# A third group of blocks in seven products in the last two gate-and-up stages, 64 instead of 48 pre-added weight blocks' transfers, and fixed PSUM banks

## The chip, the cores and the metric

The kernel runs on one core of a Trainium2 chip as a single launch. The metric is device time in microseconds. Before the change three runs took 997.59, 998.87 and 999.01 us, so the median is 998.87 us. The execution that the profiler recorded took 996.52 us, and the span from its first to its last instruction is 994.7 us.

## What is computed

Two decoder layers run on 256 tokens of width 1024 in float32. Each layer is a feed-forward net (added with factor 0.5), a token mixer (causal pooling beside attention), and a second feed-forward net. The feed-forward net is the part that the change touches:

```python
D_MODEL, SEQ, DEPTH, D_FF = 1024, 256, 2, 2816

def rms_norm(x, g):
    xf = x.astype(jnp.float32)
    y = xf * lax.rsqrt(jnp.mean(xf * xf, axis=-1, keepdims=True) + EPS)
    return (y * g.astype(jnp.float32)).astype(x.dtype)

def swiglu(h, w_gate_up, w_down):
    a, b = jnp.split(h @ w_gate_up, 2, axis=-1)
    return (jax.nn.silu(a) * b) @ w_down

    x = x + 0.5 * swiglu(rms_norm(x, ffn1_norm), ffn1_w_gate_up, ffn1_w_down)
    ...                     # the mixer
    x = x + 0.5 * swiglu(rms_norm(x, ffn2_norm), ffn2_w_gate_up, ffn2_w_down)
```

## The kernel before

**Number format.** Each float32 operand is split into two float32r parts, `hi` and `lo`. A product is made of hi by hi, hi by lo and lo by hi. Weights come from DRAM in units of 1 MB (128 partitions x 2048 floats). A unit is loaded into a tile `raw` (4 buffers) by a transfer that SP issues; ScalarE copies each half to `hi`; VectorE subtracts and writes `lo` (`split`, lines 186 to 188, for plain units; lines 176 and 177 for sum forms). `hi` and `lo` have six half-size buffers each, which is three units. A load for unit i therefore waits until the split of unit i-4 has read `raw`, and a split of unit i waits until TensorE is done with unit i-3. `unit()` hands out the next split unit, `fetch()` starts the following one.

**Stages.** There are four feed-forward stages: stage 0 (which begins the program), stage FU, stage LU and stage LU+FU. The mixer stands between 0 and FU and between LU and LU+FU. Each stage has 22 gate-and-up blocks (128 columns of the gate and 128 of the up matrix) and then 11 down units. In stage 0 every block is computed plainly: `pair` multiplies one unit with the normed activations `hx` (32 matmuls, PSUM tile `ps`), and `drain` moves the result to `ab` (one ScalarE copy, one VectorE add). `post` then scales with the norm, applies SiLU, multiplies and splits two blocks for the down product (tiles `ga`, `gb`, `gc`, `gd`).

**Seven products.** In stages FU, LU and LU+FU two groups of four blocks, A (blocks 12 to 15) and B (blocks 18 to 21), are computed in the Strassen-Winograd manner: tokens and the 1024 inputs are each halved, and seven products (`strassen`, forms "1" to "7", 16 matmuls each, `by_tokens`) stand in for the four pairs. Their left sides are the activations' halves and four sums of them (`x_forms`, made once a stage after block 2, tiles `pre`, `vt`, `sf`); their right sides are three quadrants of the weights (forms 1, 2, 3) and four sums of quadrants (7, 6, 5, 4). Results are kept by tokens in PSUM (tiles `pxA`, `pyA`, `pzA`), go through `tk`, get SiLU and product in `gated` (ScalarE writes `sg`, VectorE writes `vt`), and are turned back by TensorE transposes into `pt` in `turned` (four transposes for two blocks; a ScalarE copy and a VectorE subtraction then write `gd` or `gb`).

**Weight sums in DRAM.** The four sums of quadrants are built in DRAM by accumulating transfers on POOL's queue, ahead of their stage: `go_on` issues the next step, held back by a dependency on the last VectorE operation in the list `marks`. A group needs eight steps: for form 7 a copy and an accumulation from `w`, for form 6 a copy of sum 7 (`f<-f`) and an accumulation, for form 5 a copy and an accumulation, for form 4 a copy of sum 6 (`f<-f`) and an accumulation. Six groups make 48 steps. SP then loads a sum like a unit (`raw<-f`).

**Order.** TensorE runs in program order (`keep`); the framework's scheduler places the other engines' instructions between, and each engine runs its list in order. The order of a stage's pairs and forms is the list of `feed_order`: a number is a pair, "1A" is form 1 of group A:

```python
return [0, 1, "1A", 2, "2A", 3, 4, "7A", 5, "6A", 6, "5A", 7, "4A", "3A", 8, "1B", 9, "2B", 10, "7B", 11, "6B", 16,
        "5B", 17, "4B", "3B"]
```

After "3A" follow pair 8, the transposes for two blocks, form "1B", the first half of pair 9, the transposes of the other two blocks. PSUM tiles of the pool `pat` (4 banks) are taken in turn. The down product comes right after, and group B's transposes stand inside it.

Of the kernel before, what the change touches and what calls it, by code (L numbers as in the profile page):

```python
# [18 lines left out]
F32 = mybir.dt.float32  # L19
# [6 lines left out]
P = 128  # L26
# [17 lines left out]

FU = NF + NF // 2 + 24
LU = FU + NF + NF // 2
GROUPS = {"A": 12, "B": 18}
XF = 2
SHIFT = 16
RAW = {"1": "11", "2": "21", "3": "22"}  # L50
SUMS = (("7", "12", "22"), ("6", "7", "11"), ("5", "11", "12"), ("4", "6", "21"))


def feed_order():

    return [0, 1, "1A", 2, "2A", 3, 4, "7A", 5, "6A", 6, "5A", 7, "4A", "3A", 8, "1B", 9, "2B", 10, "7B", 11, "6B", 16,
            "5B", 17, "4B", "3B"]


def feed_units(base):  # L60
    return [base + n if isinstance(n, int) else (base, n) for n in feed_order()]


C_G1, C_GM, C_G2, C_BG, C_PS, NG = 0, 8, 16, 24, 40, 44
# [3 lines left out]
def trunk_kernel(ctx: ExitStack, tc: tile.TileContext, x_in, w_in, pw_in, qkn_in, rope_in, mask_in, band_in, out):  # L68
# [12 lines left out]
    def quarter(name):  # L81
        return pat.tile([P, 2, S], F32, name=name, tag="at")
# [64 lines left out]
        return z.rearrange("p (i c) -> p i c", i=2)  # L147

    def far_sums(base):
        steps_left.extend((base, g, f, src, kw) for g in GROUPS for f, one, two in SUMS  # L150
                          for src, kw in ((one, {}), (two, {"accum_op": OP.add})))

    def go_on():
# [241 lines left out]
    def bc2(a):  # L395
        return a.unsqueeze(1).to_broadcast([P, 2, a.shape[-1]])

    def ffn(after, n0=0, end=False, col=None, base=0, far_at=()):
        gs, gt = {}, {}

        def room(name, n0, m):
# [53 lines left out]
        if n0:  # L455
# [6 lines left out]
            for i in range(n0 + 1, NF + 1):  # L462
                if i < NF:
                    pair(unit(), wide(i))
                    fetch()
                    if i >= 8 and i % 3 == 2:
                        go_on()
                if i == NF or i % 3 != 1:
                    for n in range(done, NF if i == NF else min(done + 2, i - 1), 2):
                        scaled = post(n)  # L470
                        done = n + 2
                        if i == n0 + 1:
                            behind(scaled, drained[-1])
        else:
# [6 lines left out]
            columns(ws[1], pss[1], range(4, NK))  # L481
            drain(wide(1), pss[1])

            pre = acts.tile([P, 12 * S], F32, name="pre", tag="gb")
            vt = acts.tile([P, 2, GW], F32, name="vt", tag="v")
            tk = {g: acts.tile([P, 2, GW], F32, name="tk", tag="tok", bufs=2) for g in GROUPS}
# [56 lines left out]

            def turned(n, g):

                pt = quarter("pt")
                for i in range(2):
                    for t in range(2):
                        keep(nc.tensor.transpose(pt[:, i, t * P:(t + 1) * P], gq[2 * t + n][:, i * P:(i + 1) * P], ident))  # L549
                name, i = place(GROUPS[g] + 2 * n)  # L550
                g = gt[name][:, i:i + 2]
                act(g[:, :, 0, :], pt, AF.Copy)
                tt(g[:, :, 1, :], pt, g[:, :, 0, :].bitcast(F32), op=OP.subtract)

            bank = {}

            def strassen(f, g):

                b = ("x" if f in "1653" else "z" if f == "2" else "y") + g
                if b not in bank:  # L560
                    bank[b] = quarter("p" + b).rearrange("p a s -> p (a s)")
                z = bank[b]
# [19 lines left out]
            due = None  # L582
            wait = [0, 1]
            for n in feed_order()[2:]:
                if isinstance(n, str):
                    strassen(*n)
                    if n[0] == "3":
                        due = n[1]
                    continue
                if due == "A0":  # L590
                    pair(unit(), wide(n), lambda: turned(0, "A"), NK // 2)
                    due = None
                else:
                    pair(unit(), wide(n))
                fetch()
                if due == "A":
                    turned(1, due)
                    due = "A0"
# [8 lines left out]
            if due:  # L607
                last = {(1, 0): lambda: turned(1, due), (1, 5): lambda: turned(0, due)}
# [23 lines left out]
    def add_x(f, ps, two, r):  # L632
        t = x[:, f, :]
        if two:
            t = small.tile([P, S], F32, name="t", tag="sg", bufs=2)
            act(t, ps[:, 1, :], AF.Copy)
            if r is not None:
                tt(t, ps[:, 0, :], t, op=OP.add)
                stt(t, t, 0.5, r, op0=OP.mult, op1=OP.mult)
                marks.append(tt(x[:, f, :], x[:, f, :], t, op=OP.add))  # L640
                return
            stt(t, t, 0.5, x[:, f, :], op0=OP.mult, op1=OP.add)
        stt(x[:, f, :], ps[:, 0, :], 0.5, t, op0=OP.mult, op1=OP.add)

    def tokens():
# [362 lines left out]
    for l in range(L):  # L1008
        l_of[0] = l
        if l == 0:  # L1010
            for base in STAGES:
                far_sums(base)
        ffn(lambda f: prep(f, l, C_GM), len(w3) if l == 0 else 0, col=C_G1, base=l * LU, far_at=(1, 3, 5, 7, 9))
        if l == 0:
            for d, z in ((rope, rope_in), (mask, mask_in), (qkn, qkn_in)):
                nc.sync.dma_start(d, z)
        mix(l, lambda f: prep(f, l, C_G2))
        if l + 1 < L:
            ffn(lambda f: prep(f, l + 1, C_G1), col=C_G2, base=FU, far_at=(1, 3, 5, 7, 9))
# [92 lines left out]
```

## Time and profile before

| what | value |
|---|---|
| median of three runs | 998.87 us |
| profiled execution | 996.52 us (span 994.7 us) |
| TensorE busy | 989.5 us, 99% |
| VectorE busy | 801.1 us, 81% |
| ScalarE busy | 651.4 us, 65% |
| loads by SP, 16 DMA engines' time | 57.9% |
| transfers by POOL, 16 DMA engines' time | 21.2% |
| gate-and-up part of stage LU | from 508 to 622 us |
| gate-and-up part of stage LU+FU | from 825 to 941 us |

"Busy" is the time in which an engine executed something; on TensorE it counts overlapped matmuls as well. Durations of neighbouring instructions overlap by some hundredths of a us, so the pitch (start to start) is a little shorter than the duration. A row of the chain of waits gives start, length, engine, tile, line and the number of instructions. In a timeline row the bracket at the end is the idle time ahead of the instruction and what ended it.

### The profile page before, as it was taken

To read this page: it belongs to the slowest core of one execution; us is meant where nothing else is said; L and a number is where in the kernel's file an instruction comes from. 1 tells how busy PE (TensorE), PEld (TensorE's weight loads), DVE (VectorE), ACT (ScalarE), POOL (GpSimd) and SP (SyncE) were. 2 spreads that over 40 slices of the span, in tenths; PEclk is the share of its full clock that TensorE was granted. 3 is DMA by queue.
4 is the path that set the end of the run, shared out by engine and by line. 5 is a ranking of instruction groups with operands and counts; after the bars stand their busy time and mean duration, and the time that the engine had idled before them with its cause. 6 is when DMAs were issued, how large, how long until landed. Compare 5 with 4: busy or idle time off the path is not lost.

```text
span 994.7 us, 16119 instructions
## 1 busy us (share of the span) xinstructions
PE 989.5 (99%) x6312; PEld 898.6 (90%) x6312; DVE 801.1 (81%) x1136; ACT 651.4 (65%) x974; POOL 55.8 (6%) x95
## 2 busy tenths in 40 slices
PE   9999999999999999999999999999999999999998
PEld 8998888898899988889988889888989998888897
DVE  6987777698978799886779888676988888988862
ACT  7865555567756787675578677555677568776641
POOL 0000001002100100000000000000021000000000
PEclk9999999999999999999999999999999999999999
DMA  8878899964889999798966979897858895787740
GB/s 298 319 259 284 249 306 294 293 195 182 275 249 308 351 286 335 251 336 261 300 240 244 299 270 308 304 282 265 261 184 251 268 296 207 260 291 254 254 148 22
DMA packets 45243, 262.11 MB, mean 263 GB/s; under 512 B 4400, under 2 KB 5680, under 8 KB 22448
## 3 DMA queue, kind: packets, MB, share of 16 engines
q1 hardware_dynamic: 34992, 210.76, 57.9%
q0 software_dynamic: 10176, 50.33, 21.2%
q8 instruction: 49, 0.80, 0.3%
q14 instruction: 26, 0.21, 0.1%
HBM read 260.03 MB, written 51.38 MB: 313 GB/s over the span
## 4 chain that ended last, share of the span: by engine, by line
PE 99%; DMA 0%; ACT 0%; DVE 0%; SPq 0%; issue 0%
PE ps L99 72%; PE pt L99 7%; PE two L99 4%; PE pxB L99 3%; PE pxA L99 3%; PE pyA L99 2%; PE pyB L99 2%; PE pe L99 1%; PE sc L99 1%; PE pzB L99 1%; PE pzA L99 1%; PE pt L549 1%; PE pt L739 1%; PE y L99 1%; DMA raw<-w 0%; PE tp L695 0%
## 5 line engine op out<-in xcount | busy, mean ns | idle before, releaser
L188 DVE TENSOR_TENSOR lo<-raw,hi 128x1024 fp32r<-128x1024 f32 (+2 forms) x319 | 378.2, 1197 | 112.5 <-ACT hi L187 110.8
L187 ACT ACTIVATE hi<-raw 128x1024 fp32r<-128x1024 f32 (+2 forms) x319 | 327.8, 1036 | 198.6 <-PE ps L99 126.0
L99 PE MATMUL ps<-hx,hi 128*128 128x512 f32 x1312 | 443.2, 384 | 0.6 <-ACT hi L187 0.6
L99 PE MATMUL ps<-hx,lo 128*128 128x256 f32 x1312 | 358.7, 273 | 0.0
L99 PEld LDWEIGHTS ps<-hx,hi 128*128 128x128 f32 x1312 | 246.2, 188 | 44.6 <-ACT hi L187 0.8
L99 PEld LDWEIGHTS ps<-hx,lo 128*128 128x128 f32 x1312 | 246.5, 188 | 0.3 <-DVE lo L188 0.3
L177 DVE TENSOR_TENSOR lo<-raw,hi 128x1024 fp32r<-128x1024 f32 x84 | 102.2, 1221 | 23.8 <-ACT hi L176 23.7
L176 ACT ACTIVATE hi<-raw 128x1024 fp32r<-128x1024 f32 x84 | 88.9, 1059 | 46.8 <-PE ps L99 31.5
L99 PE MATMUL ps<-ga,hi 128*128 128x512 f32 (+1 forms) x264 | 87.9, 378 | 0.0
L99 PE MATMUL ps<-ga,lo 128*128 128x256 f32 x256 | 70.0, 273 | 0.0
L161 POOL DMA_DIRECT2D f<-w x36 | 33.3, 937 | 594.9 <-DVE ab L237 288.1
L99 PE MATMUL ps<-gb,hi 128*128 128x512 f32 (+1 forms) x198 | 65.4, 376 | 0.0
L99 PE MATMUL pt<-hi,hx 128*128 128x512 f32 x192 | 65.1, 385 | 0.0
L99 PEld LDWEIGHTS ps<-ga,hi 128*128 128x128 f32 x264 | 49.0, 188 | 8.3
L99 PE MATMUL pt<-lo,hx 128*128 128x256 f32 x192 | 52.6, 274 | 0.0
L99 PE MATMUL ps<-gb,lo 128*128 128x256 f32 x192 | 52.4, 273 | 0.0
L99 PEld LDWEIGHTS ps<-ga,lo 128*128 128x128 f32 x256 | 48.1, 188 | 0.0
L99 PE MATMUL ps<-gc,hi 128*128 128x512 f32 (+1 forms) x132 | 44.3, 376 | 0.0
L99 PE MATMUL ps<-gd,hi 128*128 128x512 f32 (+1 forms) x132 | 44.3, 376 | 0.0
L99 PE MATMUL ps<-mk,hi 128*128 128x256 f32 x256 | 44.1, 275 | 0.0
L237 DVE TENSOR_TENSOR ab<-ps,ab 128x512 f32<-128x512 f32 x62 | 42.4, 684 | 0.0
L99 PEld LDWEIGHTS ps<-gb,hi 128*128 128x128 f32 x198 | 36.7, 188 | 6.2
(251 smaller groups left out, 1585.1 us busy)
## 6 DMA issues: line engine op xcount, KB each, us to landing
raw<-w SPq DMA_DIRECT2D x170, 1024.0 KB, 6.9
f<-w POOLq DMA_DIRECT2D x36, 1024.0 KB, 11.8
raw<-f SPq DMA_DIRECT2D x24, 1024.0 KB, 5.5
raw<-w SPq DMA_DIRECT2D x16, 256.0 KB, 5.3
out_dram<-gx SPq DMA_DIRECT2D x8, 128.0 KB, 2.0
gx<-x SPq DMA_DIRECT2D x3, 256.0 KB, 5.6
qk<-pw SPq DMA_DIRECT2D x2, 256.0 KB, 4.7
gx<-x SPq DMA_DIRECT2D x1, 300.0 KB, 2.8
```

The source lines that it names most:

```text
L99: return keep(nc.tensor.matmul(*args, **kw))
L161: z = nc.gpsimd.dma_start(two_rows(far[f, g, base]), src, **kw)
L176: act(hv, a, AF.Copy)
L177: tt(lv, a, hv.bitcast(F32), op=OP.subtract)
L187: act(hi, w, AF.Copy)
L188: return tt(lo, w, hi.bitcast(F32), op=OP.subtract)
L237: drained.append(tt(t, ps[:, :, 0, :], t, op=OP.add))
L549: keep(nc.tensor.transpose(pt[:, i, t * P:(t + 1) * P], gq[2 * t + n][:, i * P:(i + 1) * P], ident))
L739: keep(nc.tensor.transpose(pt[:, h, o * P:(o + 1) * P], pr[:, h, c * P:(c + 1) * P], ident))
```

## The change

In stages LU and LU+FU a third group of four blocks (8 to 11, now called B; blocks 18 to 21 are now C) is computed in seven products. Stage FU keeps two groups, A and C. The order of a stage is a table: `TWO` for stage FU is the old order with "t1A" and "t0A" naming the transposes; `THREE` for the other two has 10 pairs and 21 forms. An entry such as `(6, "t0A")` is pair 6 with the transposes in its middle.

```diff
-GROUPS = {"A": 12, "B": 18}
+GROUPS = {"A": 12, "B": 8, "C": 18}
...
+TWO = (0, 1, "1A", 2, "2A", 3, 4, "7A", 5, "6A", 6, "5A", 7, "4A", "3A", 8, "t1A", "1C", (9, "t0A"), "2C", 10, "7C", 11, "6C",
+       16, "5C", 17, "4C", "3C")
+THREE = (0, 1, "1A", 2, "2A", 3, "1B", 4, "7A", "6A", 5, "5A", "4A", "3A", (6, "t0A"), "t1A", "7B", "6B", "2B", 7, "5B", "1C",
+         "4B", "3B", (16, "t0B"), "t1B", "7C", "6C", "2C", 17, "5C", "4C", "3C")
+FEED = {FU: TWO, LU: THREE, LU + FU: THREE}
...
-        late_r = not end
+        late_r = True
...
-                    if i >= 8 and i % 3 == 2:
+                    if i >= 8 and i % 2 == 0:
                         go_on()
...
+            three = FEED[base] is THREE
+            tk = {g: acts.tile([P, 2, GW], F32, name="tk", tag="tok", bufs=2) for g in ("AB" if three else "AC")}
+            tk.setdefault("C", tk["A"])
+            banks4 = [quarter(f"b{i}").rearrange("p a s -> p (a s)") for i in range(4)]
+            for g in groups_of(base):
+                for f in "1653":
+                    bank[f + g] = banks4[0 if (g == "B" if three else g == "A") else 2]
+                bank["2" + g] = banks4[1]
+                bank["7" + g] = banks4[3]
+                bank["4" + g] = banks4[1 if three else 3]
...
-                pt = quarter("pt")
+                if g == "C":
+                    pt = quarter("pt")
+                else:
+                    pt = banks4[1 if three or n else 0].rearrange("p (a s) -> p a s", s=S)
...
-                by_tokens(f, z, f in "127")
+                z = bank[f + g]
+                by_tokens(f, z, f in "127" or three and f == "4")
...
                 elif f == "5":
                     act(p1, z, AF.Copy)
-                    tt(p1, bank["y" + g], p1, op=OP.add)
+                    tt(p1, bank["7" + g], p1, op=OP.add)
                     gated(p1, 1, 1, 1)
+                    if three:
+                        tt(w, bank["7" + g], w, op=OP.add)
...
-                if n in (6, 11):
+                if n in steps_at:
                     go_on()
...
+        elif r is not None:
+            z = small.tile([P, S], F32, name="t", tag="sg", bufs=2)
+            stt(z, ps[:, 0, :], 0.5, r, op0=OP.mult, op1=OP.mult)
+            tt(t, t, z, op=OP.add)
+            return
...
-        ffn(..., far_at=(1, 3, 5, 7, 9))
+        ffn(..., far_at=(0, 1, 3, 4, 6, 7, 9), steps_at=(3, 6, 16))
-            ffn(lambda f: nc.sync.dma_start(out[:, f, :], x[:, f, :]), end=True, col=C_G2, base=LU + FU)
+            ffn(lambda f: nc.sync.dma_start(out[:, f, :], x[:, f, :]), end=True, col=C_G2, base=LU + FU, steps_at=(3, 6))
```

Form 4 gets a start of its own in bank 1 in the three-group stages, where it was added onto form 7's bank before; the missing sum is made up by one more VectorE addition after form 5 (line 596). Eight groups need 64 steps, and the places at which `go_on` is called now come to 64 (54 before, 48 of them used). In the last stage the norm's factor is now put on the gate half alone ahead of SiLU and on the down sums at the end, as it was in the other stages.

In the rows that follow, line numbers of the changed kernel are higher: 199 is the plain split (188 before), 188 the split of a form (177), 248 the drain (237), 562 the product in `gated` (541), 577 the split after a transpose (553), 593 and 600 the additions of forms 5 and 4 (574 and 579). `b_5315` to `b_5318` are the four fixed banks of stage LU.

VectorE's list in stage LU, from the end of `x_forms` on; before:

```order
L541 SCALAR_TENSOR_TENSOR vt<-tk,sg 128x256
L237 TENSOR_TENSOR ab<-ps,ab 128x512
L506 TENSOR_TENSOR sf<-vt,sf 128x512
L177 TENSOR_TENSOR lo<-raw,hi 128x2x2x256
L188 TENSOR_TENSOR lo<-raw,hi 128x1024 x2
```

and in the changed kernel:

```order
L562 SCALAR_TENSOR_TENSOR vt<-tk,sg 128x256
L248 TENSOR_TENSOR ab<-ps,ab 128x512
L527 TENSOR_TENSOR sf<-vt,sf 128x512
L199 TENSOR_TENSOR lo<-raw,hi 128x1024
L188 TENSOR_TENSOR lo<-raw,hi 128x2x2x256 x4
L199 TENSOR_TENSOR lo<-raw,hi 128x1024
L248 TENSOR_TENSOR ab<-ps,ab 128x512
```

Where the second half of 7A's split stood, the second half of pair 4's split stands now, and the splits of 7A and 6A follow as a run of four.

VectorE's list in stage LU around the end of group A, from the additions of form 5 or 4 to the first split after a transpose; before (the end of form 1B, pair 9 and form 2B are split in it):

```order
L579 TENSOR_TENSOR tk<-pyA,tk 128x512
L177 TENSOR_TENSOR lo<-raw,hi 128x2x2x256
L541 SCALAR_TENSOR_TENSOR vt<-tk,sg 128x256
L188 TENSOR_TENSOR lo<-raw,hi 128x1024
L541 SCALAR_TENSOR_TENSOR vt<-pxA,sg 128x256
L188 TENSOR_TENSOR lo<-raw,hi 128x1024
L443 TENSOR_TENSOR ab<-ab,r 128x2x256
L177 TENSOR_TENSOR lo<-raw,hi 128x2x2x256
L448 TENSOR_TENSOR ab<-ab 128x2x256
L177 TENSOR_TENSOR lo<-raw,hi 128x2x2x256
L237 TENSOR_TENSOR ab<-ps,ab 128x512
L553 TENSOR_TENSOR gd<-pt,gd 128x2x256
```

and in the changed kernel (pair 6 and forms 7B and 6B are split in it):

```order
L199 TENSOR_TENSOR lo<-raw,hi 128x1024 x2
L593 TENSOR_TENSOR tk<-b_5318,tk 128x512
L596 TENSOR_TENSOR tk<-b_5318,tk 128x512
L188 TENSOR_TENSOR lo<-raw,hi 128x2x2x256
L562 SCALAR_TENSOR_TENSOR vt<-tk,sg 128x256
L600 TENSOR_TENSOR tk<-b_5316,tk 128x512
L188 TENSOR_TENSOR lo<-raw,hi 128x2x2x256 x2
L562 SCALAR_TENSOR_TENSOR vt<-tk,sg 128x256
L562 SCALAR_TENSOR_TENSOR vt<-b_5317,sg 128x256
L188 TENSOR_TENSOR lo<-raw,hi 128x2x2x256
L577 TENSOR_TENSOR gd<-b_5316,gd 128x2x256
```

The product of form 4 (the second row `vt<-tk,sg`), which the first transposes read, now stands behind three halves of forms 7B and 6B.

POOL's list at its end; before (the last six rows are issued in the second mixer):

```order
L161 DMA f_7265<-w 256x1x1024
L161 DMA f_7755<-f_7265 16x16384
L161 DMA f_7755<-w 256x1x1024
L161 DMA f_7878<-w 256x1x1024 x2
L161 DMA f_8098<-f_7755 16x16384
L161 DMA f_8098<-w 256x1x1024
```

and in the changed kernel (the last two rows are issued in stage LU+FU itself, after pairs 3 and 6):

```order
L172 DMA f_8128<-w 256x1x1024 x2
L172 DMA f_8269<-f_8128 16x16384
L172 DMA f_8269<-w 256x1x1024
L172 DMA f_8414<-w 256x1x1024 x2
L172 DMA f_8860<-f_8269 16x16384
L172 DMA f_8860<-w 256x1x1024
```

The list's last transfers have moved from the mixer into a gate-and-up part.

More of the change, by code (lines that the diff above doesn't have):

```diff
@@ L51, with groups_of @@
 SUMS = (("7", "12", "22"), ("6", "7", "11"), ("5", "11", "12"), ("4", "6", "21"))
-def feed_order():
-    return [0, 1, "1A", 2, "2A", 3, 4, "7A", 5, "6A", 6, "5A", 7, "4A", "3A", 8, "1B", 9, "2B", 10, "7B", 11, "6B", 16,
-            "5B", 17, "4B", "3B"]
-def feed_units(base):
-    return [base + n if isinstance(n, int) else (base, n) for n in feed_order()]
+TWO = (0, 1, "1A", 2, "2A", 3, 4, "7A", 5, "6A", 6, "5A", 7, "4A", "3A", 8, "t1A", "1C", (9, "t0A"), "2C", 10, "7C", 11, "6C",
[3 more added lines that the diff above has]
+FEED = {FU: TWO, LU: THREE, LU + FU: THREE}
+def groups_of(base):
+    return "AC" if FEED[base] is TWO else "ABC"
+def feed_units(base):
+    for n in FEED[base]:
+        n = n[0] if isinstance(n, tuple) else n
+        if isinstance(n, int):
+            yield base + n
+        elif n[0] != "t":
+            yield base, n
 C_G1, C_GM, C_G2, C_BG, C_PS, NG = 0, 8, 16, 24, 40, 44
@@ L149, in far_sums @@
     def far_sums(base):
-        steps_left.extend((base, g, f, src, kw) for g in GROUPS for f, one, two in SUMS
+        steps_left.extend((base, g, f, src, kw) for g in groups_of(base) for f, one, two in SUMS
                           for src, kw in ((one, {}), (two, {"accum_op": OP.add})))
@@ L396, in bc2, with ffn @@
         return a.unsqueeze(1).to_broadcast([P, 2, a.shape[-1]])
-    def ffn(after, n0=0, end=False, col=None, base=0, far_at=()):
+    def ffn(after, n0=0, end=False, col=None, base=0, far_at=(), steps_at=()):
         gs, gt = {}, {}
@@ L482, in ffn @@
             drain(wide(1), pss[1])
+            bank = {}
             pre = acts.tile([P, 12 * S], F32, name="pre", tag="gb")
             vt = acts.tile([P, 2, GW], F32, name="vt", tag="v")
-            tk = {g: acts.tile([P, 2, GW], F32, name="tk", tag="tok", bufs=2) for g in GROUPS}
+            three = FEED[base] is THREE
[8 more added lines that the diff above has]
+                bank["4" + g] = banks4[1 if three else 3]
             xg = pre[:, :NK * S].rearrange("p (k s) -> p k s", s=S)
@@ L553, in turned, with seven @@
                 tt(g[:, :, 1, :], pt, g[:, :, 0, :].bitcast(F32), op=OP.subtract)
[L555 to L562, printed above, removed]
-                by_tokens(f, z, f in "127")
+            def seven(f, g):
+                z = bank[f + g]
+                by_tokens(f, z, f in "127" or three and f == "4")
                 p1, w = tk[g][:, 0], tk[g][:, 1]
@@ L580, in strassen @@
                     gated(w, 1, 0, 0)
-            due = None
             wait = [0, 1]
-            for n in feed_order()[2:]:
+            for n in FEED[base][2:]:
                 if isinstance(n, str):
-                    strassen(*n)
-                    if n[0] == "3":
-                        due = n[1]
+                    (turned if n[0] == "t" else seven)(*((int(n[1]), n[2]) if n[0] == "t" else n))
                     continue
[L590 to L594, printed above, removed]
+                n, t = n if isinstance(n, tuple) else (n, None)
+                pair(unit(), wide(n), *([lambda: turned(int(t[1]), t[2]), NK // 2] if t else ()))
                 fetch()
-                if due == "A":
-                    turned(1, due)
-                    due = "A0"
-                if n in (6, 11):
+                if n in steps_at:
                     go_on()
@@ L606, in ffn @@
             post(wait[0])
-            if due:
-                last = {(1, 0): lambda: turned(1, due), (1, 5): lambda: turned(0, due)}
+            last = {(1, 0): lambda: turned(1, "C"), (1, 5): lambda: turned(0, "C")}
         order = [divmod(b, NF) for b in (
@@ L1012, in trunk_kernel @@
                 far_sums(base)
-        ffn(lambda f: prep(f, l, C_GM), len(w3) if l == 0 else 0, col=C_G1, base=l * LU, far_at=(1, 3, 5, 7, 9))
+        ffn(lambda f: prep(f, l, C_GM), len(w3) if l == 0 else 0, col=C_G1, base=l * LU, far_at=(0, 1, 3, 4, 6, 7, 9), steps_at=(3, 6, 16))
         if l == 0:
@@ L1018, in trunk_kernel @@
         if l + 1 < L:
-            ffn(lambda f: prep(f, l + 1, C_G1), col=C_G2, base=FU, far_at=(1, 3, 5, 7, 9))
+            ffn(lambda f: prep(f, l + 1, C_G1), col=C_G2, base=FU, far_at=(0, 1, 3, 4, 6, 7, 9), steps_at=(3, 6, 16))
         else:
-            ffn(lambda f: nc.sync.dma_start(out[:, f, :], x[:, f, :]), end=True, col=C_G2, base=LU + FU)
+            ffn(lambda f: nc.sync.dma_start(out[:, f, :], x[:, f, :]), end=True, col=C_G2, base=LU + FU, steps_at=(3, 6))
 def _feat(a):
```

## The prediction

> **What bounds the kernel now.** I read the page first, then the chain of waits, then the stages by windows and VectorE's timeline. The page:
>
> ```profile
> span 994.7 us, 16119 instructions
> PE 989.5 (99%) x6312; PEld 898.6 (90%) x6312; DVE 801.1 (81%) x1136; ACT 651.4 (65%) x974; POOL 55.8 (6%) x95
> PEclk9999999999999999999999999999999999999999
> q0 software_dynamic: 10176, 50.33, 21.2%
> L187 ACT ACTIVATE hi<-raw 128x1024 fp32r<-128x1024 f32 (+2 forms) x319 | 327.8, 1036 | 198.6 <-PE ps L99 126.0
> ```
>
> TensorE is never idle and holds its full clock; ScalarE waits for TensorE to free buffers (last row), so the helpers are ahead. A change pays only if it shortens TensorE's own list, and costs whatever makes TensorE wait for the first time. VectorE is the nearest to becoming the bound. The two windows are the gate-and-up parts of stages LU and LU+FU (columns: window, length, busy time of PE, PEld, DVE, ACT, POOL, clock, DMA share, GB/s):
>
> ```profile
> 508.00:622.00 114.00, 114.00 (x687) 102.38 (x688) 101.42 (x126) 86.76 (x117) 2.90 (x4) 1.00 0.81 273
> 825.00:941.00 116.00, 116.00 (x700) 104.13 (x699) 106.52 (x127) 87.66 (x119) 0.00 (x0) 1.00 0.72 255
> ```
>
> **TensorE's gain.** From the chain, stage LU, group A (start, length, tile; pxA, pzA, pyA are forms, `ps` pairs, `pt` transposes):
>
> ```profile
> 511.00 2.72 PE pxA L99 x16
> 519.06 2.73 PE pzA L99 x16
> 521.79 10.68 PE ps L99 x64
> 532.46 2.68 PE pyA L99 x16
> 540.49 2.69 PE pxA L99 x16
> 548.53 2.68 PE pxA L99 x16
> 556.56 2.72 PE pyA L99 x16
> 559.28 2.71 PE pxA L99 x16
> 567.35 0.44 PE pt L549 x4
> 573.15 0.44 PE pt L549 x4
> ```
>
> A pair is 10.68/2 = 5.34, four are 21.36. The seven forms sum to 18.93, the two sets of transposes to 0.88. One more group gives 21.36 - 19.81 = 1.55 us; two stages give **3.1 us**. That is 0.3% of the time: a few us of waiting use it up.
>
> **VectorE's load.** Its pitches, from the timeline at the end of `x_forms`:
>
> ```profile
> 529.21 0.42 DVE L541 SCALAR_TENSOR_TENSOR vt<-tk,sg 128x256 f32<-128x256 f32 x1
> 529.55 0.68 DVE L237 TENSOR_TENSOR ab<-ps,ab 128x512 f32<-128x512 f32 x1
> 530.15 0.68 DVE L506 TENSOR_TENSOR sf<-vt,sf 128x512 fp32r<-128x512 f32 x1
> 530.75 1.22 DVE L177 TENSOR_TENSOR lo<-raw,hi 128x1024 fp32r<-128x1024 f32 x1
> 531.88 2.36 DVE L188 TENSOR_TENSOR lo<-raw,hi 128x1024 fp32r<-128x1024 f32 x2
> 534.15 1.22 DVE L177 TENSOR_TENSOR lo<-raw,hi 128x1024 fp32r<-128x1024 f32 x1
> ```
>
> So 0.34 for a product in `gated`, 0.60 for 512 columns, 1.135 for half a split ((534.15 - 531.88)/2). Three more units in a stage are 6 x 1.135 = 6.8. The group's own four additions, four products and two splits after transposes are 2.4 + 1.4 + 1.2 = 5.0; the extra additions after form 5 in A and C are 1.2; four drains and two posts go, -2.4 and -3.6. Sum +7.0: stage LU needs 101.4 + 7.0 = 108.4 of 114 - 1.55 = 112.4 us, 96%. On average it still fits. In stage LU+FU the scaling falls from 128x1024 to 128x512:
>
> ```profile
> L446 DVE TENSOR_TENSOR ab<-ab,r 128x1024 f32<-128x1024 f32 x7 | 8.5, 1220 | 0.0
> L448 DVE TENSOR_TENSOR ab<-ab 128x512 f32<-128x512 f32 x7 | 4.8, 687 | 0.4 <-ACT ab L447 0.4
> ```
>
> Seven scalings at 1.14 (8.0) become five at 0.60 (3.0); 1.2 of that difference of 5.0 is already in the two posts, so 106.5 + 7.0 - 3.8 = 109.7 of 114.4, the same share.
>
> **Where the lead runs out.** The tightest place is the first set of transposes, in the middle of pair 6. TensorE's list from form 1A (starts 511.00) to there, if it never waits: 1A, 2, 2A, 3, 1B, 4, 7A, 6A, 5, 5A, 4A, 3A, half of 6 = eight forms with 21.65 (2.72 + 2.73 + 2.72 + 2.68 + 2.69 + 2.68 + 2.72 + 2.71), four pairs with 21.36 and 2.67: due at 556.7. The transposes need form 4's product. VectorE's list ahead of it, from the split at 530.75 on (the place is unchanged, and so is the list before it), holds 18 half splits (second half of 4, all of 7A, 6A, 5, 5A, 4A, 3A, 6, 7B, first half of 6B), 8 additions of 512 columns and 2 products: 20.4 + 4.8 + 0.7 = 25.9, so 556.7 too. The margin is zero, and each us that VectorE idles in those 26 becomes a TensorE wait. Some idle is certain: 3A's second half can be split only after pair 5 has freed its buffer, at 511.00 + 29.56 + 5.34 = 545.9, and ScalarE's copy (1.06 us in a row below); that is 547.0, and VectorE would be there at 546.8 (12 half splits and 4 additions after 530.75). Other such places are met within tenths. I take 0.5 us without any late load, lower bound 0.
>
> Earlier, pair 4's second half is split until 530.75 + 1.22 = 532.0 and needed at 511.00 + 18.84 + 2.67 = 532.5: half a us to spare. The second set of transposes writes bank 1 again, after one eviction of the first, within the 2.67 us of half a pair:
>
> ```profile
> L552 ACT ACTIVATE gd<-pt 128x512 fp32r<-128x512 f32 x2 | 1.2, 588 | 0.0
> L553 DVE TENSOR_TENSOR gd<-pt,gd 128x512 fp32r<-128x512 f32 x2 | 1.4, 686 | 0.0
> ```
>
> Every other fixed bank is read at least one form (2.68) before it is written again. I price the banks at nothing, since an eviction of 1.3 us fits into each of these gaps; if its reader stands behind a split, the wait is up to 1.2 us. Queued behind a TensorE wait is all of TensorE's list; behind VectorE's, the splits of 6B and 2B.
>
> **The transfers.** After pair 3 `go_on` now issues a copy `f<-f`, after pair 6 an accumulation. What such a transfer does to loads: rows around the accumulation at 551.74 with the queues' shares from 555 to 559; the copy at 437.79 with its share from 441 to 444; the load that becomes form 5A's place; and, without any transfer, a load's time to landing (825 to 941) and the rate of loads alone (566 to 571):
>
> ```profile
> 551.74 1.03 POOL L161 DMA_DIRECT2D f<-w  x1 [63.71 <-DVE ab L237]
> 554.93 0.38 SPq L171 DMA_DIRECT2D raw<-w  x1
> 567.56 1.06 ACT L176 ACTIVATE hi<-raw 128x1024 fp32r<-128x1024 f32 x1 [4.16 <-DMA raw<-w]
> q0 software_dynamic: 164, 0.67, 97.9%
> q1 hardware_dynamic: 17, 0.03, 2.5%
> 437.79 0.52 POOL L161 DMA_DIRECT2D f<-f  x1 [15.03 <-DVE ab L237]
> q0 software_dynamic: 20, 0.98, 81.1%
> 532.04 0.33 SPq L171 DMA_DIRECT2D raw<-f  x1
> raw<-f SPq DMA_DIRECT2D x8, 1024.0 KB, 4.8
> DMA packets 297, 2.14 MB, mean 428 GB/s; under 512 B 32, under 2 KB 32, under 8 KB 40
> ```
>
> From 555 to 559 POOL's queue had 97.9% of the engines and the loads 2.5%; the load issued at 554.93 landed 12.6 us later instead of 4.8. The copy had 81.1% from 441 to 444. By the Trainium skill, "DMA: Bandwidth & Descriptors", section "SWDGE vs HWDGE vs iDMA", a DMA engine goes round-robin between its queues; a load beside a transfer would then lose about 2.5 us, an estimate, and the upper bound for an accumulation below would be about 1.2 us instead of 6.5. The trace differs: the loads were shut out for 4 us, and it decides.
>
> In the changed kernel the copy follows pair 3's drain (529.55 + 0.68); its data flows 3 us later, from 533 to 536. Form 5A's load is issued when the row 532.04 stands now, after pair 4's split, and would land at 536.8, that of 4A 2.45 later (1 MB at 428 GB/s), at 539.3. The copy pushes them back by its 2 to 3 us; 4A lands at 541.3 to 542.3 and its first half is with VectorE 1.06 later, at 542.4 to 543.4. VectorE gets there at 542.2 (nine half splits and two additions after 530.75), so it idles 0.2 to 1.2 us, in the middle 0.7. The loads behind (3A, 6, 7B) arrive before their buffers are free. The wait at the transposes is then 0.5 + 0.7 = **1.2 us per stage**, two stages **2.4 us**. Bounds: 0, and with an accumulation's 12.6 - 4.8 = 7.8 us in that place 547.1 + 1.06 - 542.2 + 0.5 = 6.5 each.
>
> The accumulation after pair 6 is issued near 561 (556.7, the transposes 0.44, half a pair 2.67, the drain); its victims are loads of 5B to 3B. There the lead is several us again, since pair 6 with the transposes takes TensorE 6.2 us and a unit's split VectorE 2.3. I take nothing, upper bound 4. SP's load of sum 4C waits for that accumulation, which lands by 574; the load is due after 580 (4C is the last form but one of some 112 us from 508), so it isn't held.
>
> The other 14 added transfers lie in stage 0, FU, the downs and the mixers. Each takes 0.212 x 994.7 / 48 = 4.4 us of DMA time; the fullest stretch is stage 0's down part:
>
> ```profile
> 122.00:182.00 60.00, 60.00 (x361) 53.97 (x360) 43.21 (x61) 32.07 (x46) 4.64 (x7) 1.00 0.94 293
> ```
>
> Two more make 0.94 + 8.8/60 = 1.09: the surplus spills into the mixer. Its cover is ScalarE, idle for 28 of these 60 us behind TensorE; if that is gone, a load comes up to 4.4 us late.
>
> **The tail.** After the last matmul one VectorE instruction sets the end:
>
> ```profile
> 991.17 0.42 DVE gx L643
> ```
>
> It becomes two: **+0.4 us**.
>
> **Sum.** 996.52 - 3.1 + 2.4 + 0.4 = 996.2 for a profiled execution, that is -0.3. The median lies 2.35 above the profiled one, so I predict 998.6.
>
> **Rivals.** *The waits stay away* (at most 0.3 per stage). For it: loads are far ahead in most of the program, and a copy is short. Against it: the zero margin. Time 998.87 - 3.1 + 0.4 + 0.3 = 996.5, faster. *Slower: POOL's transfers shut out the loads where splits stand in a run.* Place: forms 5A, 4A, 3A, where the lead is spent, and 5B, 1C, 4B, 3B. Price: 6.5 and 4 us at most; it decides once a load there lands over 7 us after issue. At 4.5 us a stage it gives 998.87 - 2.7 + 9.0 = 1005.2. For it: 97.9% in the row above. Against it: the late load of 567.56 cost TensorE nothing, with pairs between the forms. *VectorE falls behind for good*, since 96% leaves no room for its waits for ScalarE (12.6 us idle of 114 in stage LU): then the part's length is VectorE's 108.4 + 12.6 = 121 instead of 114, +7 in each stage, 1013. Against it: that idle time is TensorE's lead, not VectorE's need.
>
> **Chances.** Forecast (waits of 0.7 to 4.7 us in all) 0.47; no waits 0.26; shut-out loads 0.21; VectorE behind 0.02; a late load in another stage, 2 to 5 us, 0.04. About 0.2% (2 us) is what a measurement can tell, so faster 0.26, same 0.47, slower 0.27. The likeliest case's own range is 997 to 1001; with the others it is 996.0 to 1003.5.
>
> **What would show it.** Right: the chain stays on TensorE, with waits of about 1 us ahead of the first transposes into bank 1 (line 573) for VectorE's line 562, in LU and LU+FU alone, and 4A's load landing over 6 us after issue. Wrong: no idle TensorE at all; waits at line 110 for `lo` or `hi` in other stages; transposes with time to spare while form 5 or 3 waits for ScalarE's copy of its bank; or a chain that runs over VectorE.

## The result, and the profile after

The changed kernel takes 1003.78 us (median of five runs, 1002.66 to 1006.61) against 998.61 us for the kernel before on the same chip (996.53 to 999.01): a ratio of 1.0061 with a 95% interval of 1.0043 to 1.008. It is slower, by about 5 us where 0.3 us faster was forecast, and just above the upper end of the forecast range (1003.5). The profiled execution took 1004.64 us. Its page:

```profile
span 1002.9 us, 16181 instructions
PE 989.0 (99%) x6296; PEld 896.4 (89%) x6296; DVE 812.7 (81%) x1160; ACT 661.0 (66%) x988; POOL 69.2 (7%) x111
PEclk9999999999999999999999999999999999999999
q0 software_dynamic: 13568, 67.11, 28.1%
```

The span grew by 8.2 us while TensorE's busy time stayed, so TensorE now idles, at full clock. The view of waits of TensorE (line, what it waited for, us in total, times, longest) names the places in its first three rows:

```profile
PE b L573 <- DVE vt L562: 4.8, 3, 1.8
PE b L573 <- DVE gc L577: 2.2, 2, 1.1
PE b L110 <- ACT tk L592: 1.1, 2, 0.7
```

Line 573 is the transposes into bank 1: three of the first sets wait for VectorE's product in `gated`, two of the second sets for the eviction of the first. To see how much each stage lost, I measured in the trace from the start of a stage's sum of squares (tile `ss`) to its first down matmul; all "parts" below are this length. The two windows of LU and LU+FU (columns as in the prediction):

```profile
509.00:627.00 118.00, 112.91 (x675) 100.33 (x674) 106.19 (x133) 91.77 (x123) 3.43 (x5) 1.00 0.90 301
831.00:947.00 116.00, 112.87 (x676) 100.43 (x675) 106.53 (x133) 91.58 (x124) 2.58 (x3) 1.00 0.90 312
```

| stretch, us | before | after | difference |
|---|---|---|---|
| start to stage 0's `ss` (first loads) | 29.88 | 30.56 | +0.68 |
| part of FU | 106.35 | 106.35 | 0 |
| part of LU | 106.24 | 110.80 | +4.56 |
| part of LU+FU | 106.35 | 108.73 | +2.38 |
| stage 0's part | 93.58 | 93.58 | 0 |
| stage 0's down and the first mixer | 210.05 | 210.06 | +0.01 |
| FU's down | 67.63 | 67.63 | 0 |
| LU's down and the second mixer | 211.03 | 210.89 | -0.14 |
| LU+FU's down | 60.02 | 60.12 | +0.10 |
| last matmul to the end | 3.59 | 4.15 | +0.57 |

TensorE's own list became 1.55 us shorter in each part, so the waits cost 6.1 us in LU and 3.9 in LU+FU (4.56 + 1.55 and 2.38 + 1.55), where 1.2 each was forecast. The rest is the tail, and a beginning that varies anyway: in the thirteen profiles of this study it lies between 29.8 and 31.8.

The reference is a part in which TensorE never waits: 106.24 - 1.55 = 104.7 us in LU and 106.35 - 1.55 = 104.8 in LU+FU.

How the largest loss comes about in LU, in the timeline of SP, POOL, ScalarE and VectorE:

```profile
565.55 1.03 POOL L172 DMA_DIRECT2D f<-w  x1 [33.83 <-DVE ab L248]
...
568.14 0.38 SPq L182 DMA_DIRECT2D raw<-w  x1
571.02 0.33 SPq L143 DMA_DIRECT2D raw<-w  x1
...
582.09 2.01 ACT L187 ACTIVATE hi<-raw 128x1024 fp32r<-128x1024 f32 x2 [4.30 <-DMA raw<-w]
...
583.18 2.36 DVE L188 TENSOR_TENSOR lo<-raw,hi 128x1024 fp32r<-128x1024 f32 x2 [4.02 <-ACT hi L187]
```

The accumulation after pair 6 is issued at 565.55. Form 3B's load follows at 568.14 and pair 16's at 571.02. The view of transfers from 569 to 572 gives the queues' shares (packets, MB, share of the 16 engines; q0 is POOL's queue, q1 that of the loads) and the time from issue to landing of the load issued there; the last row is the same for the load of 568.14:

```profile
q0 software_dynamic: 93, 0.38, 79.6%
q1 hardware_dynamic: 13, 0.07, 5.2%
raw<-w SPq DMA_DIRECT2D x1, 1024.0 KB, 13.4
...
raw<-w SPq DMA_DIRECT2D x1, 1024.0 KB, 13.8
```

The loads that were outstanding (pair 16's from 571.02 on) got 5.2% of the engines. ScalarE idles 4.30 us for 3B's data, VectorE 4.02 us behind it, and the chain of waits shows where that reaches TensorE:

```profile
589.94 1.08 DVE lo L188
591.02 1.10 issue
592.13 0.42 DVE vt L562
...
596.20 0.70 DVE gc L577
596.90 0.04 issue
596.94 0.66 PE b L573 x4
```

Between 590.8 and 592.6 TensorE waits 1.8 us for form 4B's product, which stands in VectorE's list behind the late splits, and then 1.1 us for the eviction at 596.20. At t0A, at 557.5, it waits 1.7 us in the same way.

### The profile page after: what moved, and what is told of

It reads as the page before. It is cut to its first block, busy times and chain, and to the rows that moved or that the text cites. A ratio compares the mean times of both kernels' runs of the same rounds, so it can differ in the third digit from the quotient of the medians.

```text
span 1002.9 us, 16181 instructions
## 1 busy us (share of the span) xinstructions
PE 989.0 (99%) x6296; PEld 896.4 (89%) x6296; DVE 812.7 (81%) x1160; ACT 661.0 (66%) x988; POOL 69.2 (7%) x111
## 4 chain that ended last, share of the span: by engine, by line
PE 95%; DVE 3%; issue 1%; DMA 0%; ACT 0%; SPq 0%; DVEq 0%
PE ps L110 66%; PE b L110 14%; PE pt L110 7%; PE two L110 4%; DVE lo L188 1%; PE pe L110 1%; PE sc L110 1%; PE pt L755 1%; PE y L110 1%; DVE lo L199 0%; PE b L573 0%; DVE vt L562 0%; DMA raw<-w 0%; PE tp L711 0%; PE pt L573 0%
## 5 line engine op out<-in xcount | busy, mean ns | idle before, releaser
L199 DVE TENSOR_TENSOR lo<-raw,hi 128x1024 fp32r<-128x1024 f32 (+2 forms) x303 | 358.9, 1196 | 104.8 <-ACT hi L198 103.2
L110 PE MATMUL ps<-hx,hi 128*128 128x512 f32 x1184 | 401.2, 385 | 0.5 <-ACT hi L198 0.5
L110 PE MATMUL ps<-hx,lo 128*128 128x256 f32 x1184 | 324.1, 274 | 0.1
L110 PEld LDWEIGHTS ps<-hx,lo 128*128 128x128 f32 x1184 | 222.8, 188 | 0.6 <-DVE lo L199 0.6
L188 DVE TENSOR_TENSOR lo<-raw,hi 128x1024 fp32r<-128x1024 f32 x112 | 134.8, 1221 | 26.2 <-ACT hi L187 24.5
L187 ACT ACTIVATE hi<-raw 128x1024 fp32r<-128x1024 f32 x112 | 116.5, 1055 | 53.9 <-PE ps L110 26.0
L110 PE MATMUL b<-hi,sf 128*128 128x512 f32 x256 | 88.0, 385 | 1.1 <-ACT tk L592 1.1
L172 POOL DMA_DIRECT2D f<-w x48 | 44.5, 1004 | 591.8 <-DVE ab L248 232.6
L110 PE MATMUL b<-lo,sf 128*128 128x256 f32 x256 | 70.2, 274 | 0.0
L110 PE MATMUL b<-hi,hx 128*128 128x512 f32 x192 | 58.7, 386 | 0.0
L110 PEld LDWEIGHTS b<-hi,sf 128*128 128x128 f32 x256 | 48.0, 188 | 10.2 <-ACT tk L592 1.4
L110 PEld LDWEIGHTS b<-lo,sf 128*128 128x128 f32 x256 | 48.1, 188 | 0.0
```

Source lines behind the costliest of these rows:

```text
L110: return keep(nc.tensor.matmul(*args, **kw))
L172: z = nc.gpsimd.dma_start(two_rows(far[f, g, base]), src, **kw)
L187: act(hv, a, AF.Copy)
L188: tt(lv, a, hv.bitcast(F32), op=OP.subtract)
L199: return tt(lo, w, hi.bitcast(F32), op=OP.subtract)
```

## Experiments

Two theories. **Theory 1**: VectorE's list in itself is too late at the transposes (zero margin and 96% load). **Theory 2**: it would be in time, but POOL's transfers inside the two parts push loads back and VectorE idles. The parts' lengths, each from one profile, and the times (median, or one run where marked). How far a part repeats is seen where no edit touches it: stage 0's part is 93.56 to 93.60 us in all thirteen profiles; LU without transfers lies between 105.22 and 105.55 (e1, e7, e9), but LU+FU without them between 105.32 and 106.14 (e1, e9, e10, e12), and 107.22 in e7.

| kernel | FU | LU | LU+FU | time, us | ratio to before |
|---|---|---|---|---|---|
| before | 106.35 | 106.24 | 106.35 | 998.61 | |
| changed | 106.35 | 110.80 | 108.73 | 1003.78 | 1.0061 |
| e1 no transfers in LU, LU+FU | 106.43 | 105.30 | 105.70 | 995.78 | 0.999 [0.998, 0.9999] |
| e2 later transposes | 106.35 | 111.96 | 107.32 | 1001.95 | 1.0052 [1.0032, 1.0072] |
| e3 both | 106.35 | 105.93 | 106.95 | 998.11 | 1.0007 [0.9998, 1.0017] |
| e4 two groups everywhere | 106.35 | 106.24 | 106.35 | 997.23 | 1.0003 [0.9985, 1.0022] |
| e5 only the copy taken out | 107.27 | 109.67 | 109.73 | 1005.09 | 1.0073 [1.0059, 1.0087] |
| e6 one transfer, after 3 | 110.38 | 106.28 | 110.35 | 1005.66 | 1.0078 [1.0062, 1.0094] |
| e7 e1, t1 later | 106.35 | 105.55 | 107.22 | 997.43 | 0.9999 [0.9989, 1.0008] |
| e8 e4, three steps after 6 | 107.34 | 106.24 | 106.35 | 998.41 (one) | |
| e9 e1, steps earlier | 109.36 | 105.22 | 105.52 | 998.13 | 1.0003 [0.9993, 1.0014] |
| e10 e1, wide scaling in LU | 106.35 | 106.93 | 106.14 | 997.99 (one) | |
| e12 e1, accumulation after 3 of LU | 106.69 | 109.95 | 105.32 | 1000.04 (one) | |

The kernel before took 997.44 us in the runs beside e1 to e4, 997.46 beside e5 to e8 and 996.93 beside e9 to e12. The ratio compares with these.

### The transfers taken out (e1)

```diff
-            if h >= 3:
-                go_on()
+            go_on()
...
-        ffn(lambda f: prep(f, l, C_GM), ..., base=l * LU, far_at=(0, 1, 3, 4, 6, 7, 9), steps_at=(3, 6, 16))
+        ffn(lambda f: prep(f, l, C_GM), ..., base=l * LU, far_at=(0, 1, 3, 4, 6, 7, 9))
...
-            ffn(..., end=True, col=C_G2, base=LU + FU, steps_at=(3, 6))
+            ffn(..., end=True, col=C_G2, base=LU + FU)
```

Heads 0 to 2 of both mixers give a step each now; the step that stood after pair 16 of LU moves with the others.

> The changed kernel without any transfer in the gate and up parts of LU and LU+FU; the steps that stood there go to the mixers' heads 0 to 2 (one step each). Theory 1 (VectorE's list comes too late at the transposes, by its own length): the waits at line 573 stay, about 1.7 us at t0A and 1.8 at t0B in LU, 1.1 at each t1B; only the wait for form 5's copy goes; 1002.5 to 1003.5 us. Theory 2 (the transfers push the loads back): in LU the wait at t0B and at t1B goes and the one at t0A falls to about 1, in LU+FU the two waits left of it go; 997.5 to 1000.

995.78 us, faster than either theory asked for and faster than the changed kernel; against the one before it is 0.1% faster, hardly outside its interval. LU's part is 105.30 and LU+FU's 105.70. The waits in the whole program at line 573 are one row:

```profile
PE b L573 <- DVE vt L562: 0.6, 1, 0.6
```

That one is in LU+FU. The loads that answer to those of 568.14 and 571.02 were issued at 566.78 and 569.65 and needed, in the view of transfers, 6.0 and 5.6 us to landing instead of 13.8 and 13.4:

```profile
raw<-w SPq DMA_DIRECT2D x1, 1024.0 KB, 6.0
...
raw<-w SPq DMA_DIRECT2D x1, 1024.0 KB, 5.6
```

Theory 2 holds. What theory 1 claims is left with 0.6 and 0.9 us (105.30 - 104.7, 105.70 - 104.8), a tenth and a quarter of the losses of 6.1 and 3.9.

### The transposes one place later, with and without transfers (e2, e3)

```diff
-... "3A", (6, "t0A"), "t1A", "7B", "6B", "2B", ...
+... "3A", 6, "t0A", "7B", "t1A", "6B", "2B", ...
-... "3B", (16, "t0B"), "t1B", "7C", "6C", "2C", ...
+... "3B", 16, "t0B", "7C", "t1B", "6C", "2C", ...
```

> The changed kernel with the transposes one place later: t0A after pair 6 instead of in its middle, t1A after form 7B; t0B after pair 16, t1B after form 7C. Transfers as in the changed kernel. Theory 1: all waits at line 573 go, 7.0 us of idle time and some tenths behind each; 996 to 997.5 us. Theory 2: form 3B and pair 16 in LU still come late, so TensorE waits there 2 to 3 us at line 110 instead; 999 to 1001.

> Both edits together. Either theory: no wait left in the two parts but some tenths; the gain of TensorE is there: 995.5 to 997 us. A third possibility, that VectorE's load of 96% is too much whatever is moved: waits of 2 us and more at line 110 for splits; 999 or above.

Without the transfers 998.11 us, 2.3 more than e1: there the later place costs. With the transfers 1001.95 us, above both forecasts and 1.8 below the changed kernel, with intervals that overlap: no cure. The wait for the product went, and the one for the eviction grew. e2's chain of waits ahead of t1B in LU:

```profile
595.92 0.29 DVE ab L454
596.21 0.31 issue
596.52 1.23 DVE lo L188
597.75 0.60 DVE ab L248
598.35 0.61 DVE gc L577
598.96 0.04 issue
599.00 1.12 PE b L573 x4
```

After the whole pair 16 VectorE's list holds the drain of the pair ahead of the eviction of t0B, and before it a split and a scaling. With the first set in the middle of the pair, the eviction stands ahead of the drain. The forecast for e3 that both theories shared (995.5 to 997) wasn't met, since it overlooked this.

Part of e2's 111.96 us in LU is something else. Right behind this wait of 2.8 us the granted clock of TensorE (the column ahead of the last two) is 0.50 for 3.4 us, where about half, 1.7 us, is lost (an estimate), and the four transposes at its start took 1.12 us:

```profile
595.00:598.80 3.80, 1.16 (x8) 0.80 (x6) 3.80 (x5) 2.60 (x4) 0.15 (x1) 1.00 0.98 369
598.80:602.20 3.40, 3.19 (x11) 2.88 (x12) 3.40 (x5) 0.60 (x1) 0.54 (x1) 0.50 0.99 295
```

The profile of e6 shows the same twice, from 1.3 and 1.4 us behind waits of 1.9 us in FU and in LU+FU (397.5 to 400.9 and 871.9 to 875.3). Waits of 2.2 us in e12 and 2.4 in e5 had no such stretch behind them, and the changed kernel has none in its two parts.

### Two groups in all stages (e4), and more steps there (e8)

```diff
-FEED = {FU: TWO, LU: THREE, LU + FU: THREE}
+FEED = {FU: TWO, LU: TWO, LU + FU: TWO}
```

and for e8 beside it

```diff
                 if n in steps_at:
-                    go_on()
+                    for _ in range(3 if base == LU and n == 6 else 1):
+                        go_on()
```

> The changed kernel with two groups in all three stages (12 to 15 and 18 to 21, 48 held transfers), with its fixed banks, its transposes into banks 1 and 0 and its two-instruction tail. If the third group alone is what costs: before plus the tail's 0.4 to 0.6 us, 999 to 999.8 us. If the fixed banks or the new places of the transfers cost something themselves: above 1000.5.

> Two groups in all stages as in the earlier run of that kind, but three steps after pair 6 of LU in place of one. In the two-group order the lead is 5 to 8 us there, and one transfer cost nothing. If it is the lead that covers a shut-out of about 7 us, three in a row use it up: TensorE waits 3 to 10 us in LU for splits of units that were loaded late, 1000 to 1007 us. If loads get their share while transfers queue: none, 997.5.

e4: 997.23 us, as before. The parts are as long as before to 0.01 us, so the fixed banks and the transposes' banks cost nothing in this order, and its span of 995.2 ends 4.04 us after the last matmul (3.59 before): the two-instruction tail is 0.46 us. The same accumulation stands after pair 6 here, and in its wake (554 to 559) two loads needed a median of 10.3 us. TensorE has no wait at all in that part, since each split of the units loaded in that wake is ready 5 to 9 us ahead of its use. In e8 I expected three steps to use that up: wrong. LU's part is again 106.24, with loads of 12.5 us in the median from 556 to 568:

```profile
553.51 1.74 POOL L172 DMA_DIRECT2D f<-w  x2 [21.02 <-DVE ab L248]
574.15 1.03 POOL L172 DMA_DIRECT2D f<-w  x1 [18.89 <-DMA f<-w]
...
raw<-w SPq DMA_DIRECT2D x3, 1024.0 KB, 12.5
```

The third step waited for the data of an earlier one (18.89 us), so two transfers flowed in a row and not three; the test is milder than it was meant to be. FU, which the edit doesn't touch, is 1.0 us longer in this profile. The queues' shares from 558 to 561, and then from 564 to 567, show two regimes:

```profile
q0 software_dynamic: 123, 0.50, 90.6%
q1 hardware_dynamic: 12, 0.06, 5.1%
...
q0 software_dynamic: 148, 0.56, 52.0%
q1 hardware_dynamic: 147, 0.59, 50.4%
```

First the loads are shut out, later the two share by halves. The smallest lead on the way, ahead of pair 10, fell from 5.8 us in e4 to 3.9. So a load that lands some 12 us after issue costs nothing where the lead is larger than its delay: the transfer alone doesn't decide.

### The copy alone, the accumulation alone, and the two kinds in one place (e5, e6, e12)

```diff
# e5: the copy after pair 3 leaves; heads 2 to 7 give a step
+            if h >= 2:
+        ffn(..., base=l * LU, ..., steps_at=(6, 16))
+            ffn(..., base=LU + FU, steps_at=(6,))
# e6: one step in each part, after pair 3; in LU a plain transfer, in LU+FU an accumulation
+            if h >= 1 + l:
+        ffn(..., base=l * LU, ..., steps_at=(3,))
+            ffn(..., base=LU + FU, steps_at=(3,))
# e12: e1 with one step in LU, after pair 3, an accumulation
+        ffn(..., base=l * LU, ..., steps_at=(3,))
```

> The changed kernel with only the copy after pair 3 taken out of LU and LU+FU (the step goes to the mixers' head 2); the accumulations after pair 6 and the transfer after 16 in LU stay. If copy and accumulation each cost their own part: the wait at t0A falls to 0.1 in LU and 0.6 in LU+FU, the wait for form 5's copy in LU+FU (0.74) goes, those at t0B (1.8) and t1B (1.1 each) stay; the part from the stage's sum of squares to the first matmul of the down part, 110.8 and 108.7 in the changed kernel, becomes 109 and 107; 1000 to 1001 us. If the copy alone starts it all: both 105.3 to 105.7, 996 us. If the accumulations alone do: 110.8 and 108.7 stay, 1003 to 1004.

> The changed kernel with one transfer alone in each of the two parts, after pair 3: in LU a plain one from the weights (no addition), in LU+FU an accumulation. If the length of the shut-out decides and not that an addition is made: LU, 107 (the copy's 1.7 us at t0A and no other wait); LU+FU, where the transfer lasts longer, with the waits at form 5A to t0A at 3 to 6 us: 109 to 112; 1000 to 1004 us. If transfers cost only together with the one after pair 6: 105.3 and 105.7; 996.

> The kernel without transfers in the two parts, with one alone after pair 3 of LU, an accumulation. The copy in that place cost 1.0 to 1.1 us. If the length of the shut-out decides: 3 to 5 us, LU's part 108.5 to 110.5, with 5A's or 4A's load 11 us or more to landing. If an accumulation costs no more than a copy of the same size: 106.3.

In LU the three answer to one another. The plain transfer after pair 3 alone costs 106.28 - 105.30 = 1.0 us; taking the copy out of the changed kernel gains 110.80 - 109.67 = 1.1. The accumulation after pair 6 costs 109.67 - 105.30 = 4.4 (the transfer after 16 that e5 keeps has no wait behind it). An accumulation after pair 3 costs 109.95 - 105.30 = 4.65, over four times as much as the plain transfer of the same 1 MB in the same place. e12's rows: the issue, the queues' shares while it flows from 532.4 to 535.9, the loads issued in that time, ScalarE, and TensorE's waits in LU:

```profile
530.81 1.02 POOL L172 DMA_DIRECT2D f<-w  x1 [41.08 <-DVE ab L248]
...
q0 software_dynamic: 119, 0.49, 89.5%
raw<-f SPq DMA_DIRECT2D x2, 1024.0 KB, 11.1
...
543.50 2.01 ACT L187 ACTIVATE hi<-raw 128x1024 fp32r<-128x1024 f32 x2 [6.48 <-PE ps L110]
...
PE b L110 <- ACT tk L590: 2.2, 1, 2.2
PE b L573 <- DVE vt L562: 1.4, 1, 1.4
PE b L110 <- ACT tk L592: 1.0, 1, 1.0
```

and e6's for the plain transfer, with the first load behind it and TensorE's wait in LU:

```profile
535.26 0.69 POOL L172 DMA_DIRECT2D f<-w  x1 [30.81 <-DVE ab L248]
raw<-f SPq DMA_DIRECT2D x1, 1024.0 KB, 6.7
...
PE b L573 <- DVE vt L562: 1.2, 1, 1.2
```

From 532.4 to 535.9 no packet of the load queue stands in the answer. The loads of 5A (issued at 532.32) and 4A (at 534.54) needed 11.1 and 11.2 us; in e1 the two needed 4.9 and 5.9, in e6 beside the plain transfer 6.7 and 8.0. The first packet of 5A's load came 4.0 us after its issue in e12, 3.0 in e6 and 0.9 in e1: the plain transfer shuts loads out as well, but it is over sooner. It took 3.1 us of the 16 engines' time and landed after 5.8 us, the accumulation of as many bytes 6.0 us and 12.4. Two of TensorE's waits are for ScalarE's copies of a bank (L590, form 6; L592, form 5): the copy stands in ScalarE's list behind the split of the unit that came late. (ScalarE's row names TensorE as what ended its 6.48 us; the load it needs landed at 543.39, 0.1 us before it began.)

In LU+FU the accumulation after 3 gives 110.35 (e6), the one after 6 109.73 (e5), against 105.70. Both also have a wait at pair 4 that e1 doesn't have (0.45 and 1.28 us), ahead of the steps in question, and e6's part holds 3.4 us at half clock. So in LU+FU copy and accumulation are not told apart by these runs; together they cost 108.73 - 105.70 = 3.0, with an uncertainty of at least half a us by the spread above. By place, the changed kernel's idle time there is 0.74 and 1.26 us up to t0A, before the accumulation is issued, and 1.12 us at t1B behind it. The accumulation landed after 12.3 us there (16.2 in LU), its two loads after 10.9 and 10.8 (13.8 and 13.4).

I had forecast 1000 to 1001 for e5 if each transfer costs its own part (996 and 1003 to 1004 for the other cases) and 1000 to 1004 for e6. They came out at 1005.09 and 1005.66. In e5 it is mostly LU+FU, 109.73 where 107 was forecast, and FU with 0.9 more; in e6 it is FU, 110.38 instead of 106.35 (some 1.7 us of the difference by the half clock), though its order has two groups. One or two steps more in the first mixer change which step falls on which place of FU.

### Leftovers: t1 alone later, steps earlier, more work for VectorE (e7, e9, e10)

```diff
# e7: e1, with the second sets one form later
+... (6, "t0A"), "7B", "t1A", "6B", "2B", ... (16, "t0B"), "7C", "t1B", "6C", "2C", ...
# e9: e1, with two steps at the mixers' first two places
         norm_rope(q, qkn[:, l, 0])
         go_on()
+        go_on()
...
         norm_rope(k, qkn[:, l, 1])
         go_on()
+        go_on()
# e10: e1, with stage LU scaling gate and up halves
-        late_r = True
+        late_r = base != LU
```

> The kernel without transfers in the two parts (the earlier run of that kind), and t1A after form 7B, t1B after form 7C, with t0A and t0B in the middle of their pairs as in the changed kernel. If the eviction of t0 between the two is what costs the last tenths: 0.2 to 0.4 us less at each of four places, 994.8 to 995.4 us. If not, as without it, 995.8; if t1's own eviction then comes late for form 2's bank, a wait at line 110 of about 1 us, 997.

> The kernel without transfers in LU and LU+FU (first run of that kind), with two steps instead of one at the mixers' first two places, so that the last step is through some places before LU+FU begins (there it was issued 5 us before, and its data flowed into the stage until 13 us after its sum of squares). If that leftover is what spends the lead of pair 4 in LU+FU (-0.1 us) and makes the wait at t0A (0.6): the part falls from 105.7 to 105.3, 995.2 to 995.8 us. If the extra steps crowd the mixers: their stretch, 209.8 and 210.9, grows by 1 to 3 us, 997 to 999.

> The kernel without transfers in the two parts, with stage LU scaling gate and up blocks (128x1024, 1.14 us) instead of the gate block alone (128x512, 0.60): 0.54 more for VectorE in each of five scalings, two of them ahead of t0A in its list. If the margin at t0A is zero as the prediction counted it: the wait there grows from 0.1 to about 1.1 us and LU's part from 105.3 to 106.3; at t0B nothing, its lead is 3 us. If VectorE's 96% is the bound: LU longer by all of 2.7 us, 108.

e7 gained nothing: 997.43 us, LU 105.55. Where no load is late, the second sets have nothing to wait for. Its LU+FU (107.22 against 105.70) has 1.1 us of idle time at t0A and 0.3 us at pair 4, both ahead of the edited places, where e1 has 0.6 in all; so more than half of the difference isn't the edit's.

e9: LU+FU falls to 105.52, as the leftover theory says, but by 0.2 us only. FU goes up to 109.36 and eats it all, with these waits in TensorE's view, all but the first row's smaller one (0.5, in LU+FU) in FU:

```profile
PE b L573 <- DVE vt L562: 2.0, 2, 1.5
...
PE b L110 <- ACT tk L590: 0.7, 1, 0.7
```

The mixers' stretch was 210.3 and 210.9 (209.8 and 210.9 in e1), so they take two more steps each with next to no harm.

The traces show where FU's waits come from in e6 and e9, as far as a place can. In both an accumulation is issued 45 us after the stage's sum of squares, when the transfers ahead of it have only just landed (43.4 and 44.5 us); TensorE's longest waits, 1.9 and 1.5 us, follow 62 and 63 us after that sum. In the changed kernel's FU the transfer ahead had landed at 33.7 us, and the accumulation at 46.6 cost nothing. No run tests this.

e10: LU's part grew by 1.6 us (105.30 to 106.93), for 2.7 us of added work. The waits in LU:

```profile
PE ps L110 <- DVE lo L199: 1.1, 1, 1.1
PE b L573 <- DVE vt L562: 0.2, 1, 0.2
```

I had put the wait at t0A; most of it came earlier, at the first half of pair 4. The scheduler had moved that split: in e1 it ends 5.1 us ahead of its use, in e10 both halves stand in a row, from 530.33 to 532.68, and pair 4 starts at 530.2. So e10 changes VectorE's order and not its load alone. The loss is not the full 2.7: VectorE's 96% alone isn't the bound.

## Why the prediction was wrong

**TensorE's gain: right.** e1's LU is 0.94 us shorter than before with 0.6 us of lost time still in it, so the 1.55 us are there: pair 6 with its transposes took 6.64 us against 5.34 + 0.88 = 6.22, pair 16 6.38, and 0.42 + 0.16 is that 0.6.

**The zero margin at the first transposes: right.** "I take 0.5 us without any late load": e1 lost 0.6 and 0.9. Of the half us to spare at pair 4's second half, e1 had 0.4 in LU and nothing in LU+FU. e10, whose list has another order, doesn't test the margin at the transposes. VectorE's 96% alone didn't make it the bound.

**The copy after pair 3: right in kind, somewhat small.** 0.7 forecast, 1.1 measured in LU (the plain transfer of e6: 1.0).

**The accumulation after pair 6: this step failed.** The prediction said: "There the lead is several us again ... I take nothing, upper bound 4." It measured 4.4 us in LU, and with the 0.6 of the margin and the 1.1 of the copy that is LU's whole loss of 6.1. In LU+FU the loss of 3.9 is the 0.9 that e1 has as well and 3.0 for copy and accumulation. The numbers needed were in the prediction: an accumulation makes a load 12.6 - 4.8 = 7.8 us later (here 13.8 - 6.0 = 7.8; the 4.8 is of loads of sums, and by loads from `w` just ahead, which took 5.5, it is 7.0), and a lead has to be larger than that to hide it. "Several us" was never counted unit by unit: in e1 the split of form 3B is ready 3.9 us and that of pair 16 3.1 us ahead of use. The differences, 7.8 - 3.9 = 3.9 and 7.8 - 3.1 = 4.7, lie on both sides of the 4.4; about the upper bound itself was the value to take. The row of the kernel before that I let speak against it (the late load of 567.56 cost nothing) came from an order in which pairs between the forms give more lead; e4 has late loads in the same place, 5 to 9 us of lead and no wait.

**The second sets: wrong by the same step.** They were priced at nothing because an eviction fits between; without transfers that holds (e1). Behind a late load it didn't: 1.1 us at t1B in each stage, part of the losses above, and within the "up to 1.2 us" that the prediction named for a reader behind a split.

**The other transfers: right for the changed kernel** (FU, downs and mixers are as long as before), but with less margin than I said: e6's and e9's FU, 4.0 (some 1.7 of it the half clock) and 3.0 us longer, show that another distribution of the same 64 steps costs there. **The tail** was forecast at 0.4 and is 0.46 in e4, 0.57 in the changed kernel.

The rival "POOL's transfers shut out the loads where splits stand in a run", at 1005.2 us and with a chance of 0.21, was the right one in kind and nearest in time; of its two places (5A to 3A, and 5B to 3B) the second was dearer in LU. By the Trainium skill, "DMA: Bandwidth & Descriptors", section "SWDGE vs HWDGE vs iDMA", the queues take turns on an engine, which would have made a load about 2.5 us later, an estimate worked out in the prediction; the runs show 7.8, and even shares only in the transfer's later part (52.0% to 50.4% in e8). The estimate took it that a turn is short; how much a queue moves in one turn no run here shows.

Not settled: why POOL's queue takes the engines almost whole at first; what each of FU's places costs in e6 and e9; how LU+FU's 3.0 us divide; and why some waits of about 2 us are followed by half clock and others not.

## What to carry to other kernels

A background transfer is free only as far as the lead of the loads behind it: count that lead for each unit in the new order and set it against the lateness that the same kind of transfer already shows in the trace, and when the lead is the smaller, take the difference as the price, not nothing. Where an order packs work denser, move the background steps to stretches whose loads have lead to spare first; here moving them to the mixers turned 1.0061 into 0.999. Then look what the moved steps do to the other stages, and at the granted clock behind each wait of some 2 us.

## What the runs showed of the hardware

A DRAM-to-DRAM accumulation of 1 MB (e12) left a load that was issued 1.5 us after it without a packet for the next 4.0 us (0.9 without a transfer, e1), with 89.5% of the engines for POOL's queue from 532.4 to 535.9, and 139 GB/s moved. Later in such a transfer the two queues shared by halves (e8). The two loads behind it landed after 11.1 us instead of 5.4 in the median, and it cost TensorE 4.65 us. A plain transfer of the same size in the same place took half the engines' time (3.1 us instead of 6.0), held the first packet back 3.0 us, and cost 1.0.

A wait can cost more than its idle time. Within 1.4 us of waits of 1.9 (twice) and 2.8 us the granted clock fell to 0.50 for 3.4 us (e6, e2); behind waits of 2.2 and 2.4 us it stayed at 1.00 (e12, e5). In LU of the changed kernel, at full clock, the idle times of the view sum to 4.9 us (1.7, 0.3, 1.8 and 1.1) while 6.1 were lost; but e1, with 0.1 us of idle time there, lost 0.6 as well, so about half of the difference has nothing to do with these waits.
